# A decoder layer with two attention mixers: the second pair's queries and keys ahead of the transposed values, and the norm's sums inside the first pair's key product

## The chip, the cores and the metric

The kernel runs on one core of a Trainium2 chip. The metric is the device time of one execution in microseconds (us); three runs of the kernel before gave a median of 1153.85 us (1153.38 to 1154.62). The engines are named as the profile names them: PE (TensorE, matrix products; PEld is its weight load), DVE (VectorE), ACT (ScalarE), POOL (GpSimd) and SP (SyncE, which here only issues transfers). Each engine works through its own list of instructions in order and waits for others by semaphores.

## The reference, cut to what matters

```python
x = x + 0.5 * swiglu(rmsnorm(x, norm_ffn1), ffn1_gate, ffn1_up, ffn1_down)
h = rmsnorm(x, norm_mix)
qa, ka, va, qb, kb, vb, g_a, g_b = split(h @ w_in)      # 12 heads A, 8 heads B, 64 wide
# A: dilated windows, heads 0-3 (128, 1), 4-7 (512, 4), 8-11 (2048, 16); keys t - i*dilation
for each group: out, lse = dilated_window_attention(q, k, v, slopes, window, dilation)
y_a = sum(softmax(lse over the groups) * out)            # heads h, 4+h, 8+h merge into one
# B: block-sparse causal attention (at 512 positions every past block is taken)
y_b = moba_attention(qb, kb, vb, slopes)
merged = sigmoid(g_a) * (y_a @ w_up_a) + sigmoid(g_b) * (y_b @ w_up_b)
x = x + merged @ w_out
x = x + 0.5 * swiglu(rmsnorm(x, norm_ffn2), ffn2_gate, ffn2_up, ffn2_down)
return rmsnorm(x, norm_final)
```

There are 512 positions, a width of 1024 and an inner width of 2816, all float32; `rmsnorm` divides by the root of the mean square over the width and multiplies by a gain.

## The kernel before, in words

**Tiles.** The activations lie transposed: eight tiles `X[k]` of 128 features by 512 positions. A float32 product is made of three matmuls (`mac`, L205 to L210): both operands are split into a rounded high part and the rest, and high*high, high*low and low*high are summed in PSUM. One product of a 128-wide column of weights with all of `h` is eight such triples, 24 matmuls of 512 columns.

**Weights.** All weight tiles come in one list, `stream`, in the order in which the products ask for them. `fetch` loads a tile three ahead (tile `raw`, three buffers, queue of SP), `split` makes its high part on ACT (`whi`, L191) and the rest on DVE (`wlo`, L192) one tile ahead, in two buffers. A changed order of the products changes this list with them.

**The norm.** The gain is put on `X` before the products; the factor 1/root(mean square) of each position is multiplied onto the results afterwards, so products can start before it is known. `squares` sums the squares tile by tile into `SSQ`. `factors` (L245) splits the sum (`sh` on ACT, `sl` on DVE), adds over the 128 partitions by two matmuls with ones (L251, L252, into `ps_out`), and then works on DVE and ACT: mean (L256), root (L239, ACT), reciprocal (L240), a Newton step (L241, L242) and the factor as a row `rrow` (L243). `columns` (L265) takes it out as columns too.

**Queries, keys and values of the mixers.** `project` makes one product for a pair of heads, queries (j = 0) or keys (j = 1). `stacked` (L459) multiplies by `rrow` into the tile `qkv` (L466, one buffer), splits it into `qkhl` (two buffers; high part on ACT, L468, rest on DVE, L469), and copies high and low parts with SP's queue into the stacked tiles `qs` and `ks` that the scores read: four copies for queries (L480, 64x512), four for keys (L482, 64x1024). The second use of a `qkhl` buffer must wait until the copies out of it have landed. `values_by_class` (`vd`) makes a pair of the dilated heads' values, multiplies by `rrow` into `qkv` as well (L531), and `turned` transposes it by four matmuls with the identity (L541, 128x128), after which ACT and DVE split it into the tile `vd` (L544, L545). `turned` is called inside the next item's product, after 18 of its 24 matmuls (`LATER`), or, when no item follows, at the list's end.

**The order.** PE's instructions stand as the program writes them. `FIRST` lists what is done ahead of the first heads: pair 0 (heads 0 and 1, by hand, L774 to L782), then the rest of the list. `BESIDE` lists for each main stage (scores of a head, then its weighted sums) which products run beside it, mixed in by `blend`. The first head's scores (L578) need the queries and keys of pair 1 (heads 4 and 8) first, then (L590) those of pair 0; the third head's need those of pair 4 (heads 6 and 10). The lists of DVE, ACT and SP are made by a scheduler from the program's order and its own estimates.

Of the kernel before, what the change touches and what calls it, by code (L numbers as in the profile page):

```python
# [49 lines left out]
def slopes(n):  # L50
# [5 lines left out]
WAIT = 5  # L56
LEAD = 9
LATER = 5

FIRST = [("qk", 0), ("vd", 0), ("vd", 2), ("qk", 1)]
BESIDE = [
    [("qk", 2), ("v", 0)], [("qk", 3)],
    [("vd", 1), ("g", 0)], [("vd", 3), ("qk", 4), ("g", 1, 0)],
    [("qk", 5)], [("qk", 6)],
    [("g", 1, 1), ("v", 3)], [("qk", 7)],
    [("qk", 8)], [("v", 4)],
# [28 lines left out]
def decoder_layer(ctx: ExitStack, tc: tile.TileContext, xT, gains, gus, gu1, dn1, wqk, wv, wvd, wg, wup, wout, gu2, dn2, base, out):  # L97
# [11 lines left out]
    def bank(which):  # L109
        group = {"all": range(8), "acc": range(4), "att": (4, 5, 6), "out": (7,)}[which]  # L110
        n = turn[which] = turn.get(which, -1) + 1
        b = group[n % len(group)]
        return psum.tile([P, 512], F32, tag=f"b{b}", name=f"ps_{which}_{n}")

    def f32(ap):
        return ap.bitcast(F32)
# [26 lines left out]
    def mixer_tiles(what, n, *js):  # L143
        src = {"qk": lambda j: wqk[2 * n + j], "v": lambda j: wv[max(0, n - 2), j], "vd": lambda j: wvd[n], "g": lambda j: wg[2 * n + j]}[what]
        return [((what, n, j), src(j)) for j in js or range(1 if what == "vd" else 2)]

    def down_tiles(i, dn):
        return [((i, "d", m, c), dn[m][:, cut]) for m in range(KT) for c, cut in enumerate(CHUNKS)]
# [3 lines left out]
    stream += down_tiles(0, dn1)  # L152
    stream += [tile for items in [FIRST] + BESIDE for item in items for tile in mixer_tiles(*item)]
    for m in range(KT):
# [41 lines left out]
    def weights(*key):  # L196

        t = state["at"]
        assert stream[t][0] == key, (t, stream[t][0], key)
        state["at"] += 1  # L200
        split(t + 1)
        fetch(t + 3)
        return splits.pop(t)

    def mac(ps, w, x, first, last):  # L205

        (wh, wl), (xh, xl) = w, x
        nc.tensor.matmul(ps, wh, xh, start=first, stop=False)  # L208
        nc.tensor.matmul(ps, wh, xl, start=False, stop=False)  # L209
        nc.tensor.matmul(ps, wl, xh, start=False, stop=last)  # L210

    def cols(w, k, n=P):
        return w[0][:, k * n:(k + 1) * n], w[1][:, k * n:(k + 1) * n]
# [23 lines left out]
    def newton(y, z, a, out):  # L237

        nc.scalar.activation(y, a, AF.Sqrt)  # L239
        nc.vector.reciprocal(y, y)  # L240
        nc.vector.scalar_tensor_tensor(z, y, -0.5, y, ALU.mult, ALU.mult)  # L241
        nc.vector.tensor_tensor(z, z, a, ALU.mult)  # L242
        nc.vector.scalar_tensor_tensor(out, z, 1.5, y, ALU.add, ALU.mult)  # L243

    def factors(i, ps):  # L245

        sh = tpool.tile([P, S], F32R, name="sh", tag="fg")
        sl = tpool.tile([P, S], F32R, name="sl", tag="fu")
        nc.scalar.copy(sh, SSQ[i])
        nc.vector.tensor_tensor(sl, SSQ[i], f32(sh), ALU.subtract)  # L250
        nc.tensor.matmul(ps, ones_r, sh, start=True, stop=False)  # L251
        nc.tensor.matmul(ps, ones_r, sl, start=False, stop=True)  # L252
        a = tpool.tile([P, S], F32, name="mean", tag="fg")
        y = tpool.tile([P, S], F32, name="root", tag="fu")
        z = tpool.tile([P, S], F32, name="step", tag="ssq", bufs=1)
        nc.vector.tensor_scalar(a, ps, 1.0 / D, EPS, ALU.mult, ALU.add)  # L256
        row = tpool.tile([P, S], F32, name="rrow", tag="rrow", bufs=1)
        newton(y, z, a, row)
        return row

    def columns(row):

        rest = tpool.tile([P, P], F32, name="rest", tag="fu")
        for t in range(NT):
            nc.vector.tensor_tensor_reduce(rest, row[:, t * P:(t + 1) * P], ident, 1.0, 0.0, ALU.mult, ALU.max,  # L265
                                           accum_out=rcol[:, t:t + 1])
        return rcol
# [167 lines left out]
    with ExitStack() as mix:  # L435
        op = mix.enter_context(tc.tile_pool(name="op", bufs=2))
        att = ExitStack()
# [10 lines left out]
        R = {}  # L448
        Q, K = {}, {}

        def project(t, j, which="acc"):

            w = weights("qk", t, j)
            ps = bank(which)
            for k in range(KT):
                mac(ps, cols(w, k), XN[k], k == 0, k == KT - 1)
                yield ps

        def stacked(t, j, ps):  # L459
            v = tpool.tile([P, S], F32, name="qkv", tag="ssq", bufs=1)  # L460

            dilated = PAIRS[t][0] in range(NT, NA)
            to, x, r = v, ps, R["row"]
            if dilated:
                to, x, r = v.rearrange("p (r i) -> p r i", r=NT), by_class(x), by_class(r)
            nc.vector.scalar_tensor_tensor(to, x, -0.125 if j == 0 else 1.0, r, ALU.mult, ALU.mult)  # L466
            hl = mp2.tile([P, 2, S], F32R, name="qkhl", tag="qkhl", bufs=2)
            nc.scalar.copy(hl[:, 0], v)  # L468
            nc.vector.tensor_tensor(hl[:, 1], v, f32(hl[:, 0]), ALU.subtract)  # L469

            for n, h in enumerate(PAIRS[t]):
                s = slice(n * HD, (n + 1) * HD)
                if j == 0:
                    Q[h] = op.tile([P, S], F32R, name="qs", tag="qs", bufs=6)
                else:
                    K[h] = op.tile([P, 2, S], F32R, name="ks", tag="ks", bufs=6)
                for half in range(2):
                    d = slice(half * HD, (half + 1) * HD)
                    if j == 0:
                        nc.sync.dma_start(f32(Q[h][d]), f32(hl[s, half]))  # L480
                    else:
                        nc.sync.dma_start(f32(K[h][d]), f32(hl[s]))  # L482
# [53 lines left out]
        def turned():  # L536

            n, vt = TURN.pop()
            pt = bank("att")
            for r in range(NT):  # L540
                nc.tensor.transpose(pt[:, r * P:(r + 1) * P], vt[:, r * P:(r + 1) * P], ident)  # L541
            v = mp.tile([P, NT, 2, P], F32R, name=f"vd{n}", tag=f"vd{n}", bufs=1)
            x = pt.rearrange("p (r h c) -> p r h c", r=NT, h=2)
            nc.scalar.copy(v[:, :, :, :HD], x)  # L544
            nc.vector.tensor_tensor(v[:, :, :, HD:], x, f32(v[:, :, :, :HD]), ALU.subtract)  # L545
            for h in range(2):
                for r in range(NT):
                    V[r, 4 + 2 * n + h] = v[:, r, h]
# [203 lines left out]
        def part(what, n, *js):  # L752

            if what == "qk":
                return qk_pair(n), 2 * KT
            if what == "v":
                return values(n), NT * KT
            if what == "vd":
                return values_by_class(n), KT
            js = js or range(2)  # L760
            return (step for j in js for step in gate(n, j)), len(js) * KT

        def parts(items):

            for item in items:
                for at, _ in enumerate(part(*item)[0]):
                    if at == LATER and TURN:
                        turned()
                    yield
            if TURN:  # L770
                turned()
# [1 line left out]

        early = []  # L774
        for j in range(2):
            for ps in project(0, j, "att"):
                pass
            early.append(ps)
        R["row"] = factors(1, bank("out"))
        R["col"] = columns(R["row"])  # L780
        for j in range(2):
            stacked(0, j, early[j])  # L782
        for _ in parts(FIRST[1:]):
            pass
# [47 lines left out]
        for m in range(KT):  # L832
            w = weights("out", m)
            ps = bank("acc")
# [92 lines left out]
```

## Time and profile before

| | |
|---|---|
| median of three runs | 1153.85 us |
| the profiled execution | 1152.99 us |
| its span, first to last instruction | 1151.1 us |
| PE busy | 1126.2 us (98%) |
| DVE, ACT busy | 600.7 us (52%), 413.1 us (36%) |
| granted TensorE clock, mean | 0.990 |

The profile is of one execution. Times in it count from the span's start. A timeline row has the start, the duration, engine, line, operation, out<-in with buffer numbers left out, and in brackets how long the engine had been idle and what ended that. Matmuls overlap: the distance between two starts, not the duration, is what a row costs. [...] First layer half: to 366 us; mixers: about 366 us on.

### The profile page before, as it was taken

How to read it: one execution, taken by the hardware profiler on the slowest of the kernel's cores; microseconds unless marked ns; L12 is line 12 of the kernel's file. 1: busy time of each engine (PE TensorE's matmuls, PEld its weight loads, DVE VectorE, ACT ScalarE, POOL GpSimd, SP SyncE). 2: the span in 40 equal slices, each digit the busy share in tenths (PEclk: the TensorE clock that was granted, in tenths of full speed). 3: DMA queues.
4: the chain of work that ended last, by engine and by line, in shares of the span. 5: the costliest groups of instructions: out<-in, count | busy, mean ns of one | idle time of the engine just before them, and what ended most of it. 6: DMA issues, size and time to landing. Idle time of an engine off the chain costs nothing.

```text
span 1151.1 us, 13539 instructions
## 1 busy us (share of the span) xinstructions
PE 1126.2 (98%) x5332; PEld 944.4 (82%) x5332; DVE 600.7 (52%) x968; ACT 413.1 (36%) x637; POOL 20.0 (2%) x34
## 2 busy tenths in 40 slices
PE   9999999999999879999999999999999999999997
PEld 7888888888888659878998888888888888888886
DVE  6744444433333546757677667754744444433223
ACT  5432232222223234444455445433422322322222
POOL 0000000000000000000000000000000000000001
PEclk9999999999999889999999999999999999999999
DMA  6222322233333444436354212332223222333321
GB/s 220 92 92 99 102 92 95 99 91 101 101 89 127 128 127 131 128 110 169 109 162 128 74 65 83 114 106 92 92 97 103 93 93 100 101 86 98 101 83 73
DMA packets 37711, 122.14 MB, mean 106 GB/s; under 512 B 4880, under 2 KB 4880, under 8 KB 37648
## 3 DMA queue, kind: packets, MB, share of 16 engines
q1 hardware_dynamic: 37072, 120.08, 33.4%
q10 hardware_dynamic: 576, 1.20, 0.3%
q8 instruction: 42, 0.69, 0.2%
q14 instruction: 21, 0.17, 0.0%
HBM read 103.44 MB, written 2.10 MB: 92 GB/s over the span
## 4 chain that ended last, share of the span: by engine, by line
PE 95%; DVE 2%; DMA 2%; issue 0%; SPq 0%; ACT 0%; DVEq 0%; ACTq 0%
PE ps_all L208 20%; PE ps_all L210 20%; PE ps_all L209 20%; PE ps_acc L208 8%; PE ps_acc L210 8%; PE ps_acc L209 8%; PE ps_all L280 2%; PE ps_out L680 2%; PE ps_att L208 1%; PE ps_att L210 1%; PE ps_att L661 1%; PE ps_att L209 1%; DMA ks<-qkhl 1%; PE ps_att L636 1%; DMA raw<-in_wqk_dram 0%
## 5 line engine op out<-in xcount | busy, mean ns | idle before, releaser
L191 ACT CAST whi<-raw 128x1024 fp32r<-128x1024 f32 (+2 forms) x201 | 202.9, 1011 | 558.8 <-PE ps_all L209 255.0
L192 DVE TENSOR_TENSOR wlo<-raw,whi 128x1024 fp32r<-128x1024 f32 (+2 forms) x202 | 236.2, 1171 | 163.8 <-ACT whi L191 163.7
L210 PE MATMUL ps_all<-xh,wlo 128*128 128x512 f32 x672 | 261.5, 389 | 0.0
L209 PE MATMUL ps_all<-xl,whi 128*128 128x512 f32 x672 | 261.5, 389 | 0.0
L208 PE MATMUL ps_all<-xh,whi 128*128 128x512 f32 x672 | 261.5, 389 | 0.0
L209 PEld LDWEIGHTS ps_all<-xl,whi 128*128 128x128 f32 x672 | 126.1, 188 | 26.3
L210 PEld LDWEIGHTS ps_all<-xh,wlo 128*128 128x128 f32 x672 | 126.1, 188 | 26.1
L208 PEld LDWEIGHTS ps_all<-xh,whi 128*128 128x128 f32 x672 | 126.1, 188 | 26.1
L208 PE MATMUL ps_all<-ah,whi 128*128 128x512 f32 (+1 forms) x374 | 141.2, 378 | 0.0
L209 PE MATMUL ps_all<-al,whi 128*128 128x512 f32 (+1 forms) x374 | 140.8, 377 | 0.0
L210 PE MATMUL ps_all<-ah,wlo 128*128 128x512 f32 (+1 forms) x374 | 140.8, 377 | 0.0
L208 PE MATMUL ps_acc<-xh,whi 128*128 128x512 f32 x304 | 125.3, 412 | 0.0
L209 PE MATMUL ps_acc<-xl,whi 128*128 128x512 f32 x304 | 120.7, 397 | 0.0
L210 PE MATMUL ps_acc<-xh,wlo 128*128 128x512 f32 x304 | 120.6, 397 | 0.0
L294 DVE TENSOR_TENSOR fu<-ps_all,rrow 128x512 f32<-128x512 f32 x44 | 30.4, 690 | 124.2 <-PE ps_all L210 124.1
L208 PEld LDWEIGHTS ps_all<-ah,whi 128*128 128x128 f32 x374 | 70.4, 188 | 13.0
L209 PEld LDWEIGHTS ps_all<-al,whi 128*128 128x128 f32 x374 | 70.4, 188 | 12.9
L210 PEld LDWEIGHTS ps_all<-ah,wlo 128*128 128x128 f32 x374 | 70.4, 188 | 12.9
L292 DVE TENSOR_TENSOR fg<-ps_all,rrow 128x512 f32<-128x512 f32 x44 | 30.4, 690 | 79.8 <-PE ps_all L210 79.7
L210 PEld LDWEIGHTS ps_acc<-xh,wlo 128*128 128x128 f32 x304 | 58.2, 191 | 13.1
L209 PEld LDWEIGHTS ps_acc<-xl,whi 128*128 128x128 f32 x304 | 58.7, 193 | 8.5
L208 PEld LDWEIGHTS ps_acc<-xh,whi 128*128 128x128 f32 x304 | 58.5, 193 | 8.6
(169 smaller groups left out, 1186.6 us busy)
## 6 DMA issues: line engine op xcount, KB each, us to landing
raw<-in_gu_dram SPq DMA_DIRECT2D x84, 512.0 KB, 3.4
raw<-in_dn_dram SPq DMA_DIRECT2D x32, 512.0 KB, 3.5
raw<-in_wqk_dram SPq DMA_DIRECT2D x20, 512.0 KB, 3.5
ks<-qkhl SPq DMA_DIRECT2D x40, 256.0 KB, 4.8
raw<-in_wg_dram SPq DMA_DIRECT2D x16, 512.0 KB, 3.5
raw<-in_dn_dram SPq DMA_DIRECT2D x16, 384.0 KB, 3.1
qs<-qkhl SPq DMA_DIRECT2D x40, 128.0 KB, 2.4
raw<-in_wout_dram SPq DMA_DIRECT2D x8, 512.0 KB, 3.4
```

What stands on the lines that cost most here:

```text
L191: nc.scalar.copy(hi[:, s], raw[:, s])
L192: nc.vector.tensor_tensor(lo[:, s], raw[:, s], f32(hi[:, s]), ALU.subtract)
L208: nc.tensor.matmul(ps, wh, xh, start=first, stop=False)
L209: nc.tensor.matmul(ps, wh, xl, start=False, stop=False)
L210: nc.tensor.matmul(ps, wl, xh, start=False, stop=last)
L280: nc.tensor.matmul(ps[j], w[:, at:at + P], x, start=k == 0 and n == 0, stop=k == KT - 1 and n == 2)
L292: nc.vector.tensor_tensor(g, ps[0], R, ALU.mult)
L294: nc.vector.tensor_tensor(u, ps[1], R, ALU.mult)
L636: nc.tensor.matmul(ps[:, :n], Q[NA + h][:, i * P:(i + 1) * P], K[NA + h][:, part, :n], start=part == 0, stop=part == 1)
L661: nc.tensor.transpose(pt[:, n * P:(n + 1) * P], block, ident)
L680: nc.tensor.matmul(to(po), V[v], x[:, first:first + n], start=done == 1, stop=done == 2 * n_products)
```

## The change

It changes three places. `FIRST` now has pair 1's queries and keys right behind pair 0's, and the two products of transposed values (`vd` 0 and 2) behind them. In the stage of the second head's weighted sums, pair 4 stands ahead of `vd` 3. And `factors` is called inside pair 0's key product, after its second triple (`SUMS = 1`, counted from 0), not behind it. Nothing is added or taken out; both programs have 5106 rows in PE's list.

```diff
-FIRST = [("qk", 0), ("vd", 0), ("vd", 2), ("qk", 1)]
+SUMS = 1
+FIRST = [("qk", 0), ("qk", 1), ("vd", 0), ("vd", 2)]
 BESIDE = [
     [("qk", 2), ("v", 0)], [("qk", 3)],
-    [("vd", 1), ("g", 0)], [("vd", 3), ("qk", 4), ("g", 1, 0)],
+    [("vd", 1), ("g", 0)], [("qk", 4), ("vd", 3), ("g", 1, 0)],
...
         early = []
         for j in range(2):
-            for ps in project(0, j, "att"):
-                pass
+            for at, ps in enumerate(project(0, j, "att")):
+                if (j, at) == (1, SUMS):
+                    R["row"] = factors(1, bank("out"))
             early.append(ps)
-        R["row"] = factors(1, bank("out"))
         R["col"] = columns(R["row"])
```

Line numbers after the list rise by one (L541 becomes L542). PE at the two matmuls with ones, first before, then after; `ps_att_2592` is pair 0's key product, `ps_acc_2667` the product that follows it.

```order
L209 MATMUL ps_att_2592<-xl_7_2531,whi 128x512
L210 MATMUL ps_att_2592<-xh_7_2530,wlo 128x512
L251 MATMUL ps_out_2617<-sh,ones_r 128x512
L252 MATMUL ps_out_2617<-sl,ones_r 128x512
L208 MATMUL ps_acc_2667<-xh_0_1880,whi 128x512
```
```order
L210 MATMUL ps_att_2592<-xl_1_1973,whi 128x512
L211 MATMUL ps_att_2592<-xh_1_1972,wlo 128x512
L252 MATMUL ps_out_2599<-sh,ones_r 128x512
L253 MATMUL ps_out_2599<-sl,ones_r 128x512
L209 MATMUL ps_att_2592<-xh_2_2065,whi 128x512
```

The two rows with ones moved ahead by 18 rows, from behind the key product to its second triple; `xh_1` is the operand of that triple.

DVE, from pair 0's keys on, first before, then after. `ps_att_2592` is pair 0's keys; before, `ps_acc_2667` and `ps_acc_2700` are the transposed values and `ps_acc_2741` pair 1's queries; after, `ps_acc_2667` and `ps_acc_2709` are pair 1's queries and keys, and `ps_acc_2751` the first values.

```order
L466 SCALAR_TENSOR_TENSOR qkv<-ps_att_2592,rrow 128x512
L469 TENSOR_TENSOR qkhl<-qkv,qkhl 128x512
L531 TENSOR_TENSOR qkv<-ps_acc_2667,rrow 128x512
L545 TENSOR_TENSOR vd_2724<-ps_att_2719,vd_2724 128x8x64
L531 TENSOR_TENSOR qkv<-ps_acc_2700,rrow 128x512
L192 TENSOR_TENSOR wlo<-raw,whi 128x1024
L545 TENSOR_TENSOR vd_2765<-ps_att_2760,vd_2765 128x8x64
L466 SCALAR_TENSOR_TENSOR qkv<-ps_acc_2741,rrow 128x512
```
```order
L467 SCALAR_TENSOR_TENSOR qkv<-ps_att_2592,rrow 128x512
L470 TENSOR_TENSOR qkhl<-qkv,qkhl 128x512
L467 SCALAR_TENSOR_TENSOR qkv<-ps_acc_2667,rrow 128x512
L193 TENSOR_TENSOR wlo<-raw,whi 128x1024
L470 TENSOR_TENSOR qkhl<-qkv,qkhl 128x512
L467 SCALAR_TENSOR_TENSOR qkv<-ps_acc_2709,rrow 128x512
L470 TENSOR_TENSOR qkhl<-qkv,qkhl 128x512
L532 TENSOR_TENSOR qkv<-ps_acc_2751,rrow 128x512
L193 TENSOR_TENSOR wlo<-raw,whi 128x1024
L546 TENSOR_TENSOR vd_2808<-ps_att_2803,vd_2808 128x8x64
```

The splits of pair 1 (L467, L470) now stand right behind those of pair 0, and the first values' multiplication (L532) behind the split of pair 1's keys.

PE at the transposes, first before (inside the second values' product), then after (both, up to the first triple of pair 2's queries, `ps_acc_2833`).

```order
L209 MATMUL ps_acc_2700<-xl_5_2345,whi 128x512
L210 MATMUL ps_acc_2700<-xh_5_2344,wlo 128x512
L541 MATMUL ps_att_2719<-ident,qkv 128x128 x4
L208 MATMUL ps_acc_2700<-xh_6_2437,whi 128x512
L209 MATMUL ps_acc_2700<-xl_6_2438,whi 128x512
L210 MATMUL ps_acc_2700<-xh_6_2437,wlo 128x512
```
```order
L211 MATMUL ps_acc_2784<-xh_5_2344,wlo 128x512
L542 MATMUL ps_att_2803<-ident,qkv 128x128 x4
L209 MATMUL ps_acc_2784<-xh_6_2437,whi 128x512
L210 MATMUL ps_acc_2784<-xl_6_2438,whi 128x512
L211 MATMUL ps_acc_2784<-xh_6_2437,wlo 128x512
L209 MATMUL ps_acc_2784<-xh_7_2530,whi 128x512
L210 MATMUL ps_acc_2784<-xl_7_2531,whi 128x512
L211 MATMUL ps_acc_2784<-xh_7_2530,wlo 128x512
L542 MATMUL ps_att_2819<-ident,qkv 128x128 x4
L209 MATMUL ps_acc_2833<-xh_0_1880,whi 128x512
```

The first transposes still stand behind 18 rows of another product, now that of the second values (`ps_acc_2784`); the second ones, which stood 18 rows into pair 1's queries, stand directly behind the product whose result they read.

## Rows read from the trace of the kernel before

**Rows 1.** The page, parts 1 and 5: busy times; the weights' split on DVE.
```profile
PE 1126.2 (98%) x5332; PEld 944.4 (82%) x5332; DVE 600.7 (52%) x968; ACT 413.1 (36%) x637; POOL 20.0 (2%) x34
...
L192 DVE TENSOR_TENSOR wlo<-raw,whi 128x1024 fp32r<-128x1024 f32 (+2 forms) x202 | 236.2, 1171 | 163.8 <-ACT whi L191 163.7
```
**Rows 2.** Waits of PE, whole span: who for whom, us in total, times, longest.
```profile
PE ps_att L578 <- DMA ks<-qkhl: 9.1, 3, 6.1
PE ps_att L541 <- DVE qkv L531: 5.6, 1, 5.6
```
**Rows 3.** Timeline of PE: start, duration, line, operation; idle before it.
```profile
377.40 0.39 PE L251 MATMUL ps_out<-sh,ones_r 128*128 128x512 f32 x1
...
377.85 0.39 PE L208 MATMUL ps_acc<-xh,whi 128*128 128x512 f32 x1
...
387.15 0.39 PE L210 MATMUL ps_acc<-xh,wlo 128*128 128x512 f32 x1
...
393.17 1.09 PE L541 MATMUL ps_att<-ident,qkv 128*128 128x128 f32 x4 [5.64 <-DVE qkv L531]
...
400.83 0.60 PE L541 MATMUL ps_att<-ident,qkv 128*128 128x128 f32 x4
...
419.12 0.55 PE L578 MATMUL ps_att<-ks,qs 128*128 128x256 f32 x1 [1.48 <-DMA ks<-qkhl]
...
424.39 0.40 PE L578 MATMUL ps_att<-ks,qs 128*128 128x256 f32 x2
...
506.28 0.40 PE L210 MATMUL ps_acc<-xh,wlo 128*128 128x512 f32 x1
...
508.89 0.36 PE L578 MATMUL ps_att<-ks,qs 128*128 128x256 f32 x1 [1.54 <-DMA ks<-qkhl]
...
513.19 0.40 PE L578 MATMUL ps_att<-ks,qs 128*128 128x256 f32 x2
...
1140.36 0.61 PE L352 MATMUL ps_all<-ones,sql 128*128 128x1 f32 x4 [0.96 <-ACT sql L348]
```
**Rows 4.** Timelines of DVE and ACT, 366 to 442 us.
```profile
370.75 0.69 DVE L250 TENSOR_TENSOR sl<-ssq,sh 128x512 fp32r<-128x512 f32 x1 [0.69 <-ACT sh L249]
...
378.05 0.69 DVE L256 TENSOR_SCALAR mean<-ps_out 128x512 f32<-128x512 f32 x1 [3.77 <-PE ps_out L252]
...
380.78 3.35 DVE L240 RECIPROCAL root<-root 128x512 f32<-128x512 f32 x1 [0.90 <-ACT root L239]
...
386.64 0.68 DVE L243 SCALAR_TENSOR_TENSOR rrow<-step,root 128x512 f32<-128x512 f32 x1
...
391.25 0.69 DVE L469 TENSOR_TENSOR qkhl<-qkv,qkhl 128x512 fp32r<-128x512 f32 x1 [0.68 <-ACT qkhl L468]
...
391.98 1.05 DVE L531 TENSOR_TENSOR qkv<-ps_acc,rrow 128x512 f32<-128x512 f32 x1
...
396.86 1.08 DVE L531 TENSOR_TENSOR qkv<-ps_acc,rrow 128x512 f32<-128x512 f32 x1 [1.25 <-PE ps_acc L210]
...
390.60 0.62 ACT L468 CAST qkhl<-qkv 128x512 fp32r<-128x512 f32 x1 [1.58 <-DVE qkv L466]
```
**Rows 5.** Tile `ks`, stretches 391.9 to 395 and 411 to 414.4: issues; issue to landing.
```profile
L482 SPq DMA_DIRECT2D ks<-qkhl x4: 462/599/1206, 392.0 to 393.8; - x4
...
DMA to landing us min/median/max: 2.9/4.1/4.8
...
L482 SPq DMA_DIRECT2D ks<-qkhl x4: 461/698/1170, 411.1 to 413.2; - x4
...
DMA to landing us min/median/max: 4.7/5.5/5.9
```
**Rows 6.** Stretches: length, busy time (instructions) of five engines, granted clock, DMA share, GB/s.
```profile
420.00:425.00 5.00, 5.00 (x16) 3.96 (x15) 1.05 (x4) 1.21 (x3) 0.00 (x0) 0.59 0.00 0
...
510.00:512.00 2.00, 2.00 (x8) 1.63 (x7) 1.11 (x5) 0.94 (x3) 0.00 (x0) 0.50 0.04 8
...
1141.00:1142.00 1.00, 1.00 (x10) 1.00 (x10) 0.69 (x3) 0.20 (x1) 1.00 (x2) 1.00 0.56 217
```
## The prediction, made before the changed kernel was run

> **What bounds the kernel now.** I read the busy times first: PE is busy for 98% of the span [rows 1], so only two things can give time back, moments in which PE waits and stretches in which its clock is low. The list of PE's waits came next. Two are large, and both lie where the mixers begin: the transposes wait 5.6 us for the multiplied values, and the scores wait 9.1 us in three places for the copied keys [rows 2]. Then the timeline of PE between the first product that the change moves and the second row of scores. At full clock a row of 512 columns costs 0.227 us: from 377.85 to 387.15 there are 41 starts in 9.30 us [rows 3]. From 377.85 to the scores at 424.39 PE has 120 such rows (four products of 24 and the 24 rows of pair 2's queries), two groups of transposes (0.4 us each, an estimate between the 0.23 of their 4 x 128 columns and the 0.60 of the undisturbed group's duration) and one pair of 256-column scores (0.23). That is 27.2 + 0.8 + 0.2 = 28.2 us of work, and it took 46.5 us [rows 3]: 18.3 us too many. 13.2 of them are the waits (5.6, and 9.1 less the 1.5 of the wait at 508.89 [rows 2, 3]); the other 5 are work at a low clock, as after the second wait, where 420 to 425 was granted 0.59 [rows 6]. [...] So 22.3 us are to be had at most, and the change touches all of them.
>
> **The sums.** They stand at 377.40; 18 rows earlier is 373.3. Their input `sl` is ready at 370.75 + 0.69 = 371.4 [rows 3, 4], so PE doesn't wait and has 1.9 us to spare. Both rows remain, so PE's first moved product still starts at 377.85. The mean could start 4.1 us earlier than 378.05; I allow 0.2 for the weight split that DVE's list has ahead of it, and take 3.9. Between the mean and the row factor there is one weight split in either order (before, it stood ahead of L243, now behind the reciprocal), so the factor comes at 386.64 - 3.9 = 382.7 and the chain behind it moves alike [rows 4].
>
> **Pair 0's and pair 1's splits.** Pair 0's keys were split at 391.25 + 0.69 = 391.9 [rows 4]. 3.9 earlier is 388.1; one more weight split, 1.17 us on average [rows 1], now stands between, so 389.3. Then their four copies start. Before, the first was issued at 392.0 and the last landed at 393.8 + 4.8 = 398.6, 6.6 later [rows 5]; so they land at 395.9. This matters now and didn't before: there are two `qkhl` buffers, pair 1's queries and keys follow at once, and the cast of pair 1's keys must wait until pair 0's keys have left the same buffer. Its input is there sooner (the key product ends at 377.85 + 48 x 0.227 = 388.7, and the multiplications and the weight split ahead of it on DVE are through by about 393.5), so the copies decide. Cast 0.62 [rows 4], split 0.69 and 0.1 of hand-overs: 397.3. Queued behind that split on DVE is the first values' multiplication, for which PE's transposes wait: 1.05 us and 0.14 of hand-over, as between 391.98 and 393.17 [rows 3, 4], gives 398.5. PE reaches those transposes at 377.85 + 90 x 0.227 = 398.3. The 5.6 us become 0.2. The price of this step can't be below nothing, since a wait is no gain; its upper end, from the slower set of copies, 413.2 + 5.9 - 411.1 = 8.0 us [rows 5], is 1.6. I take 0.2, since that set had a weight load directly ahead of it in SP's list and pair 0's, as now, had its queries' copies.
>
> [...]
>
> **The second transposes.** These are a new wait, and a firm one: nothing stands between the second values' product and the transposes of its result. It is 0.16 (the last row's 0.39 less the 0.23 to the next start), 0.05, the multiplication's 1.08 [rows 4] and 0.14: 1.4 us. PE has nothing else in its list meanwhile. Its bounds are 1.2 and 1.6, by the two durations and the hand-overs; I take 1.4.
>
> **The first scores.** PE has 6 rows left after the first transposes, then waits 1.4, transposes again and does 12 rows of pair 2's queries: 398.5 + 0.4 + 1.4 + 1.4 + 0.4 + 2.7 = 404.8. Pair 1's keys are split at 397.3; with 6.6 us they are all there at 403.9, with 8.0 at 405.3 [rows 5]. A weight load stands ahead of them in SP's list, so I take 8.0: 0.5 us of wait in place of 7.6, with 0 as the other end. Behind it the 24 rows of pair 2's queries run at full clock.
>
> **The third head.** Pair 4's keys are finished 24 rows and a group of transposes earlier, 24 x 0.227 + 0.4 = 5.8 us. The scores asked for them at about 506.5 and got them at 508.9 [rows 3]; now they land near 503. The wait and the low clock behind it, 4.0 us, go, with over 3 us to spare. What moves behind is `vd` 3, whose values are first read by the third head's sums, a stage later; its split and the gate's multiplication come later on DVE, which may hold the first scores' rows there by 0 to 1 us. I take 0, since PE has three banks to go on with.
>
> **The sum.** 22.3 less 0.2, 1.4 and 0.5 is 20.2 us. Against the profiled execution's 1152.99 us (the span of 1151.1 and 1.9 around it) that gives 1132.8; the median of the runs was 0.86 above the profiled one, so I predict 1133.7 us.
>
> **Rivals.**
> 1. The short wait is enough to lower the clock. For it: the wait at the third head, 2.3 us with a short pair of scores inside it, was followed by 0.50 at 510 to 512; against it: after 0.96 us without work at 1140.36 the next stretch had 1.00 [rows 3, 6]. 1.4 lies between. Price: what low clock cost behind the two waits, 4.0 - 2.3 = 1.7 at the third head, and 424.39 - 419.12 less 0.1 and 12 x 0.227 = 2.4 at the first [rows 3]; the result would be 1135.4 to 1136.1. [...] No row here shows a wait of 1.4 us.
> 2. The copies of pairs 0 and 1, now close together on one queue, land late. Pair 0's by 8.0 instead of 6.6 adds 1.4 at the transposes and passes on to pair 1's; with the low clock of rival 1 added, since the first wait is then 1.6 and the second follows, 1135 to 1138. For it speaks that sixteen copies and two weight loads now follow one another in SP's list; against it, that pair 0's keys have hardly more directly ahead of them than before.
> 3. The third head's wait stays or a DVE queue takes its place: + 4.0, 1137.7. Against it speak the 3 us to spare.
> 4. The change doesn't do what it says at the sums: the factor is no earlier, since DVE or ACT is held by the weight splits. Then pair 0's keys land at 399.8, all behind them comes 3.9 later, with some 2 us of low clock: 1139.6.
> 5. Slower: pair 1's key split on DVE and ACT, waiting for pair 0's copies, holds the values, the weight splits and so all of PE. Each us by which the copies land after 395.7 costs one; it loses in the end only if they land 20 us after that, 26.8 us after their first issue. Rows have 6.6 and 8.0.
>
> **How the numbers follow.** Forecast 55% (its own range 1132.5 to 1135), rival 1 20%, rival 2 13%, rival 3 7%, rival 4 3%, rival 5 2%. Low end: all of 22.3 but the firm 1.4 is 1133.0 by the median, less 2 us for what the counted rows may miss: 1131. High end: rivals 1 to 4 reach 1139.6, so 1140. This kernel tells a change from none at about 0.2%, 2.3 us: every case but the last is faster by more. So faster 97%, same 1%, slower 2%.
>
> **What would show it.** In the profile after: the matmuls with ones at 373.3 without a wait, the row factor near 382.7; the cast of pair 1's keys beginning when pair 0's last copy lands, near 396; transposes near 398.5 with little wait and again near 401.7 with 1.4; the first scores complete near 405.3 instead of 419.1; a granted clock of 1.00 from 377 to 425; no wait at the third head's scores, and the rest shifted by the same amount. I am wrong if the first transposes wait over 2 us, if the clock falls to 0.50 behind the second, or if the distance from the row at 377.85 to the second row of scores is above 32 us.

## The result, and the profile after

The changed kernel took 1132.96 us, the median of four runs (1132.74 to 1133.19); the kernel before, run beside it, 1153.62 us (1153.14 to 1154.62). The ratio is 0.982, with a 95% interval of 0.9803 to 0.9837. The prediction was 1133.7 us with a range of 1131.0 to 1140.0, and faster with a chance of 0.97: right in sign, in size and in most of its steps. One term was too small by 1.1 us and another too large by 0.5. Of the experiments below, one execution of the kernel with the second transposes later took 1889.27 us at a mean granted clock of 0.557 and is left out of that kernel's median.

The page, part 1 (busy us, share of the span, instructions), against [rows 1]:

```profile
PE 1119.1 (99%) x5332; PEld 939.4 (83%) x5332; DVE 600.8 (53%) x968; ACT 413.7 (37%) x637; POOL 20.0 (2%) x34
```

The span is 1131.1 us (1151.1 before). No engine has more or less to do; PE's 1126.2 became 1119.1, mainly because its rows at half clock are gone (some 5 us at the mixers' beginning and 1.7 at the third head, by the prediction's count). The waits of PE, which answer to [rows 2] (who for whom, us in total, times, longest):

```profile
PE ps_att L542 <- DVE qkv L532: 2.3, 2, 1.2
PE ps_all L422 <- DVE wide L128: 1.5, 1, 1.5
```

Of 14.7 us in four places, 2.3 in two are left; PE no longer waits for keys. (The second row is at the program's start, and was there before.) The timeline of PE, which answers to [rows 3]. The zero point of this execution lies 0.74 us differently: the first moved product starts at 377.11 and not at 377.85.

```profile
372.58 0.39 PE L252 MATMUL ps_out<-sh,ones_r 128*128 128x512 f32 x1
...
377.11 0.39 PE L209 MATMUL ps_acc<-xh,whi 128*128 128x512 f32 x1
...
397.29 0.39 PE L211 MATMUL ps_acc<-xh,wlo 128*128 128x512 f32 x1
398.82 0.63 PE L542 MATMUL ps_att<-ident,qkv 128*128 128x128 f32 x4 [1.14 <-DVE qkv L532]
...
400.43 0.40 PE L211 MATMUL ps_acc<-xh,wlo 128*128 128x512 f32 x1
402.00 0.66 PE L542 MATMUL ps_att<-ident,qkv 128*128 128x128 f32 x4 [1.17 <-DVE qkv L532]
...
405.25 0.40 PE L579 MATMUL ps_att<-ks,qs 128*128 128x256 f32 x2
...
408.23 0.40 PE L579 MATMUL ps_att<-ks,qs 128*128 128x256 f32 x2
...
490.38 0.40 PE L579 MATMUL ps_att<-ks,qs 128*128 128x256 f32 x2
...
493.19 0.39 PE L579 MATMUL ps_att<-ks,qs 128*128 128x256 f32 x2
```

From the first moved product to the second row of scores it is 408.23 - 377.11 = 31.1 us where it was 46.5: 15.4 gained. From there to the fourth scores of the third head it is 493.19 - 408.23 = 85.0 us where it was 513.19 - 424.39 = 88.8 [rows 3]: 3.8 gained. That is 19.3 of the 20.0 us between the spans; the other 0.7 is the earlier start of this stretch, ahead of every edit. (In the eleven kernels of this study, equal up to there, `sl` starts between 370.02 and 370.75.) Stretches of the changed kernel (length, busy time of five engines, granted clock, DMA share, GB/s), which answer to [rows 6]:

```profile
388.00:396.00 8.00, 8.00 (x37) 6.63 (x36) 4.29 (x5) 1.68 (x2) 0.00 (x0) 1.00 0.97 251
398.00:403.00 5.00, 3.02 (x17) 2.37 (x18) 4.63 (x5) 1.95 (x3) 0.00 (x0) 1.00 0.90 216
403.00:425.00 22.00, 22.00 (x144) 20.09 (x143) 12.54 (x31) 10.37 (x23) 1.01 (x3) 1.00 0.58 172
490.00:495.00 5.00, 5.00 (x29) 4.23 (x27) 4.63 (x14) 1.95 (x7) 0.00 (x0) 1.00 0.32 105
```

The clock is 1.00 in all of them, also in the 5 us that hold both waits. How the first wait arises is read on DVE, ACT and the copies, which answer to [rows 4, 5]. DVE first:

```profile
381.97 0.69 DVE L244 SCALAR_TENSOR_TENSOR rrow<-step,root 128x512 f32<-128x512 f32 x1
...
387.63 0.69 DVE L470 TENSOR_TENSOR qkhl<-qkv,qkhl 128x512 fp32r<-128x512 f32 x1 [0.69 <-ACT qkhl L469]
...
396.82 0.69 DVE L470 TENSOR_TENSOR qkhl<-qkv,qkhl 128x512 fp32r<-128x512 f32 x1 [2.40 <-ACT qkhl L469]
397.62 1.05 DVE L532 TENSOR_TENSOR qkv<-ps_acc,rrow 128x512 f32<-128x512 f32 x1
```

ACT, the cast of pair 1's keys:

```profile
396.17 0.62 ACT L469 CAST qkhl<-qkv 128x512 fp32r<-128x512 f32 x1 [3.56 <-DMA ks<-qkhl]
```

Tile `ks`, the stretch of pair 0's four copies (386 to 392):

```profile
L483 SPq DMA_DIRECT2D ks<-qkhl x4: 461/712/1165, 388.3 to 390.4; - x4
...
DMA to landing us min/median/max: 4.5/5.3/5.7
```

The same for pair 1's (396 to 401):

```profile
L483 SPq DMA_DIRECT2D ks<-qkhl x4: 462/620/1164, 397.5 to 399.4; - x4
...
DMA to landing us min/median/max: 2.9/4.1/4.9
```

Read from the end: the transposes at 398.82 wait for the values' multiplication at 397.62, which stands in DVE's list behind the split of pair 1's keys at 396.82; that one waits for ACT's cast at 396.17, and the cast for pair 0's copies, the last of which was issued at 390.4 and landed 5.7 later, at 396.1. The chain is the predicted one. The copies took 7.7 us from the first issue (up to rounding), where 6.6 was planned.

### The profile page after: what moved, and what is told of

It reads as the page before. It is cut to its first block, busy times and chain, and to the rows that moved or that the text cites. A ratio compares the mean times of both kernels' runs of the same rounds, so it can differ in the third digit from the quotient of the medians.

```text
span 1131.1 us, 13533 instructions
## 1 busy us (share of the span) xinstructions
PE 1119.1 (99%) x5332; PEld 939.4 (83%) x5332; DVE 600.8 (53%) x968; ACT 413.7 (37%) x637; POOL 20.0 (2%) x34
## 4 chain that ended last, share of the span: by engine, by line
PE 96%; DVE 2%; DMA 1%; issue 0%; ACT 0%; SPq 0%; DVEq 0%; ACTq 0%
PE ps_all L210 21%; PE ps_all L209 21%; PE ps_all L211 21%; PE ps_acc L209 8%; PE ps_acc L211 8%; PE ps_acc L210 8%; PE ps_all L281 2%; PE ps_out L681 2%; PE ps_att L662 1%; PE ps_att L210 1%; PE ps_att L209 1%; PE ps_att L211 1%; PE ps_att L637 1%; DMA ks<-qkhl 1%; PE ps_all L422 0%
```

## The experiments

My theory for the time gained: three edits, each of which takes away waits and the low clock behind them, of which the sums matter mainly together with the new order. My theory for the 2.3 us left: the first wait is the buffer of `qkhl` held by pair 0's copies, the second is only PE having nothing else in its list.

**The swap alone.**

```diff
-    [("vd", 1), ("g", 0)], [("vd", 3), ("qk", 4), ("g", 1, 0)],
+    [("vd", 1), ("g", 0)], [("qk", 4), ("vd", 3), ("g", 1, 0)],
```

> The kernel before with one edit of the change alone: pair 4 ahead of the third transposed values in the stage of the second head's sums; the beginning of the mixers stays as it was. If the third head's wait was only a matter of order, the scores at 508.9 no longer wait, the granted clock there is 1.00 instead of 0.50, and all of the 4.0 us counted there are gained: about 1149.7. Rival A: the wait goes, but a row of DVE behind it becomes late (the gate's and the values' splits move back), and it costs up to 1 us: 1150.7. Rival B: the stage was covered anyway and the time stays within 0.5 us of 1153.6. The 5.6 and 7.6 us of wait at the mixers' beginning should be unchanged in all three.

1149.13 us against 1153.18, ratio 0.9967 (0.9955 to 0.9978): 4.05 us gained, 4.0 expected. PE's waits at the mixers' beginning stay (5.7 us for `qkv`, 7.8 for `ks`), and the third head's is gone, with a full clock there:

```profile
505.00:508.00 3.00, 3.00 (x17) 2.58 (x16) 2.90 (x6) 0.30 (x2) 0.00 (x0) 1.00 0.40 137
508.00:513.00 5.00, 5.00 (x27) 4.22 (x26) 4.28 (x18) 4.24 (x13) 0.00 (x0) 1.00 0.07 26
```

Neither a wait at the scores nor a stall of DVE takes its place. Its gain is about the same alone as in the changed kernel (3.8 us by the trace), so it is taken as independent of the others below.

**The sums alone.**

```diff
+                if (j, at) == (1, SUMS):
+                    R["row"] = factors(1, bank("out"))
             early.append(ps)
-        R["row"] = factors(1, bank("out"))
```

> The kernel before with only the two matmuls with ones moved 18 rows ahead. My theory: the row factor comes 3.9 us earlier, the wait of the first transposes falls from 5.6 to about 1.7, a wait of that length does not lower the clock (none of 1.2 us did in the changed kernel), so some 2.3 us of low clock behind it go too: 6.2 us, about 1147.4. The 7.6 us of wait for pair 1's keys stay, since they hang on when their product ends and not on the factor. Rival A: the wait for the keys grows by what is gained ahead of it, because the keys' split hangs on DVE's and ACT's lists, which did not begin earlier: within 1 us of 1153.6. Rival B: 1.7 us of wait is enough to lower the clock: only 3.9 us are gained, about 1149.7.

1150.0 us against 1153.18, ratio 0.9974 (0.9964 to 0.9983): 3.2 us gained, half of my 6.2. Rival A is false, since the wait for the keys did not grow (6.0 us in its longest, 6.1 before). Rival B is nearest in time, but its reason was not tested, because the wait is not 1.7. The waits:

```profile
PE ps_att L579 <- DMA ks<-qkhl: 9.2, 3, 6.0
PE ps_att L542 <- DVE qkv L532: 2.8, 1, 2.8
```

DVE in this kernel shows why 2.8:

```profile
382.25 0.69 DVE L244 SCALAR_TENSOR_TENSOR rrow<-step,root 128x512 f32<-128x512 f32 x1
...
384.46 1.22 DVE L193 TENSOR_TENSOR wlo<-raw,whi 128x1024 fp32r<-128x1024 f32 x1
...
387.90 0.69 DVE L470 TENSOR_TENSOR qkhl<-qkv,qkhl 128x512 fp32r<-128x512 f32 x1 [0.68 <-ACT qkhl L469]
```

A weight split of 1.22 us now lies between the factor and the split of pair 0's keys (from the start of one to the other 5.65 us, 391.25 - 386.64 = 4.61 before [rows 4]). The prediction had counted this split; my expectation forgot it. And 2.8 us of wait still brought the low clock:

```profile
391.00:394.00 3.00, 3.00 (x8) 2.32 (x8) 1.95 (x3) 1.11 (x2) 0.00 (x0) 0.50 1.00 243
```

So 2.8 of the 5.6 us of wait went, and hardly any of the low clock behind it.

**The first products' order alone.**

```diff
-FIRST = [("qk", 0), ("vd", 0), ("vd", 2), ("qk", 1)]
+FIRST = [("qk", 0), ("qk", 1), ("vd", 0), ("vd", 2)]
```

> The kernel before with only the order of the first products changed (pair 1 ahead of the transposed values); the sums stay late and the third head keeps its order. My theory: pair 0's keys are split 3.9 us later than in the changed kernel, so the split of pair 1's keys and the first values come 3.9 later: the first transposes wait 1.3 + 3.9 = 5.2 us, the clock falls behind them (some 2.3 us), the second transposes still wait about 1.3, the scores not at all or under 1 us, and the third head keeps its 4.0: 1133.0 + 3.9 + 2.3 + 4.0 = 1143.2. If the three edits add up, the gains are 4.0 + 6.2 + 10.4 = 20.6 of the 20.7 measured. Rival A: the edits overlap (without the early sums this order only moves the 7.6 us of wait from the scores to the transposes): less than 5 us, over 1148.5. Rival B: this order alone does nearly all (the late factor has slack behind pair 1's 48 rows): under 1139.

1144.19 us against 1153.18, ratio 0.9924 (0.9908 to 0.9941): 9.0 us gained, 10.4 expected, and both rivals missed. PE:

```profile
402.24 1.09 PE L541 MATMUL ps_att<-ident,qkv 128*128 128x128 f32 x4 [4.51 <-DVE qkv L531]
...
407.04 1.11 PE L541 MATMUL ps_att<-ident,qkv 128*128 128x128 f32 x4 [1.15 <-DVE qkv L531]
...
412.21 0.40 PE L578 MATMUL ps_att<-ks,qs 128*128 128x256 f32 x2
```

The first wait is 4.5 (5.2 expected), the second 1.15, the first scores don't wait. From the first transposes to the first scores it is 412.21 - 402.24 = 10.0 us, and 6.4 in the changed kernel: 3.5 us of low clock, where I had put 2.3:

```profile
403.00:411.00 8.00, 6.85 (x20) 5.06 (x19) 3.58 (x4) 3.50 (x4) 0.00 (x0) 0.50 0.64 172
```

The clock, once down, stayed down across the second wait and for the rows behind it. The three edits alone gain 4.05 + 3.2 + 9.0 = 16.2 us, together 20.7. The missing 4.4 is what the sums do only under the new order. There they are worth 1144.19 - 4.05 - 1132.96 = 7.2 us, with the swap's gain as it was alone: the wait of 4.5 becomes 1.14, behind which the clock no longer falls, and the 3.5 us of low clock go as a whole. Alone they gave 3.2: 5.6 became 2.8, and behind 2.8 the clock still fell.

**What holds the first transposes: a third buffer.** (To make room, a table of constants is cut to what is used and an unused tile left out.)

```diff
-            hl = mp2.tile([P, 2, S], F32R, name="qkhl", tag="qkhl", bufs=2)
+            hl = mp2.tile([P, 2, S], F32R, name="qkhl", tag="qkhl", bufs=3)
```

> The changed kernel with a third buffer for the split queries and keys (a table of constants is cut to what is used, and an unused 40-column tile is left out, so that it fits). My theory: the wait of the first transposes, 1.14 us in the changed kernel, comes from the cast of pair 1's keys, which waits until pair 0's key copies have left the buffer. With a third buffer the cast waits for pair 0's queries alone, which leave at 391.8: split near 394.7, first values multiplied by 396.5, PE there at 397.5, so no wait; the second transposes keep 1.2. About 1.2 us less than the changed kernel, 1131.8. Rival: DVE's and ACT's backlog of weight splits, not the copies, holds the values; then the wait stays near 1.1 and the time at 1133.0.

1132.15 us (1131.92 to 1132.38), ratio to the kernel before 0.9817 (0.9804 to 0.983). DVE, split of pair 1's keys and first values:

```profile
393.32 0.69 DVE L470 TENSOR_TENSOR qkhl<-qkv,qkhl 128x512 fp32r<-128x512 f32 x1 [0.73 <-ACT qkhl L469]
394.11 1.07 DVE L532 TENSOR_TENSOR qkv<-ps_acc,rrow 128x512 f32<-128x512 f32 x1
```

PE, both transposes:

```profile
397.89 0.60 PE L542 MATMUL ps_att<-ident,qkv 128*128 128x128 f32 x4
...
401.04 0.66 PE L542 MATMUL ps_att<-ident,qkv 128*128 128x128 f32 x4 [1.16 <-DVE qkv L532]
```

The split comes 3.5 us earlier although the copies landed as late as before (396.1), and the first wait is gone while the second stays. The distance from the sums to the second scores fell from 35.65 us in the changed kernel to 34.38. The theory holds; the rival, that DVE's and ACT's backlog holds the values, does not.

**The tiles' places alone**, without the third buffer.

```diff
-    cpool.tile([P, 40], F32, name="round")
-        consts = mp.tile([P, 1344], F32, name="consts", tag="consts")
+        consts = mp.tile([P, 1288], F32, name="consts", tag="consts")
```

> The changed kernel with only the cut of the constants and the tile left out that the third buffer needs: every tile behind them lies at another place in the memory, no instruction differs. Expected: the time and the waits of the changed kernel, 1133.0, first transposes 1.1, second 1.2. Rival: the places of the tiles matter by themselves (over 0.5 us either way), and the runs with a third buffer can't be read without this one.

1133.63 us (1133.27 to 1134.11), ratio 0.983 (0.9817 to 0.9843). The waits are 0.9 and 1.2, the distance from the sums to the second scores 35.49: at the place in question 0.2 us changed. The 0.67 us above the changed kernel stand elsewhere; the stretch begins 0.35 later, and whether the rest is the spread of the runs or the tiles' places was not told apart. The third buffer is faster than this kernel by 1.5 us.

**The second transposes later.**

```diff
-        def parts(items):
+        def parts(items, rest=True):
...
-            if TURN:
+            if rest and TURN:
                 turned()
...
-        for _ in parts(FIRST[1:]):
+        for _ in parts(FIRST[1:], False):
```

> The changed kernel with the second transposes taken from directly behind the product whose result they read to 18 rows later, inside pair 2's queries. My theory: their wait (1.17 us) is only PE having nothing else in its list meanwhile, so it goes and nothing takes its place: about 1.2 us less, 1131.8. Rival: the first scores, which come 1.2 us earlier for it, then wait for pair 1's keys (these landed 1.0 us before PE reached them in the changed kernel), and 0.2 us or more of it is given back, up to all of it if the copies come later: 1132.0 to 1133.0.

1132.90 us, the median of five runs (1132.16 to 1135.94), ratio 0.9829 (0.9816 to 0.9842): as the changed kernel. PE:

```profile
398.92 0.63 PE L542 MATMUL ps_att<-ident,qkv 128*128 128x128 f32 x4 [0.63 <-DVE qkv L532]
...
404.82 0.36 PE L579 MATMUL ps_att<-ks,qs 128*128 128x256 f32 x1 [1.05 <-DMA ks<-qkhl]
406.40 0.60 PE L542 MATMUL ps_att<-ident,qkv 128*128 128x128 f32 x4
```

The second transposes no longer wait, but the scores wait 1.05 us for pair 1's keys: the rival. The second wait had been covering these copies. The first wait, 0.63 us, differs from the 1.14 of the changed kernel although the edit does not touch what it waits for; the table behind the last experiment shows why.

**Both.** The edits are the two above.

> Both edits, the third buffer and the later second transposes. My theory: no wait of PE is left at the mixers' beginning; the two gains add up, 2.4 us less than the changed kernel, 1130.6, which beats both kernels. Rival: with both, PE reaches the first scores 2.4 us earlier, ahead of pair 1's copies (landed 1.0 us before PE got there); unless the copies come earlier too, 1.4 us of wait stands there and the time is that of one edit alone, 1131.8.

1131.2 us (1131.03 to 1132.14), ratio 0.9811 (0.9798 to 0.9824), the fastest of all: 1.8 us under the changed kernel, 2.4 under the one with the tiles' places alone. PE:

```profile
373.21 0.39 PE L252 MATMUL ps_out<-sh,ones_r 128*128 128x512 f32 x1
...
398.18 0.60 PE L542 MATMUL ps_att<-ident,qkv 128*128 128x128 f32 x4
...
402.74 0.40 PE L579 MATMUL ps_att<-ks,qs 128*128 128x256 f32 x2
404.36 0.60 PE L542 MATMUL ps_att<-ident,qkv 128*128 128x128 f32 x4
...
406.18 0.40 PE L579 MATMUL ps_att<-ks,qs 128*128 128x256 f32 x2
```

There is no wait left at the mixers' beginning. From the sums to the second scores it is 406.18 - 373.21 = 33.0 us, 2.7 less. The third buffer also sets pair 1's copies free earlier (issued from 395.9 on, landed at 402.6), just ahead of the scores, so the later transposes now pay.

**Why pair 0's copies took 7.7 us: another queue.**

```diff
-                        nc.sync.dma_start(f32(K[h][d]), f32(hl[s]))
+                        (nc.scalar if t == 0 else nc.sync).dma_start(f32(K[h][d]), f32(hl[s]))
```

> The changed kernel with pair 0's four key copies issued by ACT, on a queue of their own, instead of by SP. In the changed kernel the last of them landed 7.7 us after the first was issued, behind a weight load and two query copies on SP's queue. Theory A, the order of the one queue: without anything ahead of them they land about 2 us after their issue and 1.08 us apart, so near 393.5 to 394; the cast of pair 1's keys, the values and the first transposes follow and their 1.14 us of wait go: 1131.8. Theory B, the DMA engines are full (their share was 0.97 from 388 to 396): all of it has to go through whatever the queue, so the last copy lands at 396 +- 0.5 as before, the wait stays at 1.1 and the time at 1133.0 or a little above it, since ACT now issues (3 us of its list, beside waits that it has anyway).

1136.55 us, ratio 0.9856 (0.9839 to 0.9872): slower than the changed kernel. Tile `ks`, 386 to 392:

```profile
L483 ACTq DMA_DIRECT2D ks<-qkhl x4: 519/664/1178, 388.6 to 390.6; - x4
...
DMA to landing us min/median/max: 4.4/5.1/7.1
```

The last copy landed at 390.6 + 7.1 = 397.7, 9.1 us after the first issue: later, not sooner. Theory A is false. (Beside its 2 us from issue to landing: in the changed kernel the eight 256 KB stores of the result took 2.2 us in the median, and none of the copies into `ks` took under 2.9.) Theory B's reason holds, since the DMA share was 1.00 from 388 to 396, but not its numbers: it had the last copy at 396 +- 0.5 and a wait of 1.1 us. One thing more had changed: SP, rid of the copies, issued the next weight load at 390.84 (395.15 in the changed kernel), and this landed 5.6 us later, at 396.4, ahead of the last copy. That this load is what held up the last copy is likely, but was not tested by itself. PE's first transposes:

```profile
400.41 0.63 PE L542 MATMUL ps_att<-ident,qkv 128*128 128x128 f32 x4 [2.49 <-DVE qkv L532]
```

The stretch of the copies, and the one with both transposes:

```profile
388.00:396.00 8.00, 8.00 (x37) 6.62 (x36) 4.54 (x5) 1.68 (x2) 0.00 (x0) 1.00 1.00 268
400.00:404.00 4.00, 2.42 (x15) 1.86 (x15) 3.64 (x5) 1.63 (x2) 0.00 (x0) 1.00 0.94 214
```

In the profiled execution, 1134.57 us at a mean clock of 0.999, the clock stayed at 1.00 behind that wait of 2.49 us; the other three took 1136.15 to 1137.26 at 0.995 to 0.998. That the same wait lowered their clock is likely, but not shown, since they have no trace.

**The weight load among the copies.** One load is cut to an eighth.

```diff
-                nc.sync.dma_start(raws[t][:, :n], src)
+                c = n // 8 if stream[t][0] == ("qk", 2, 1) else n
+                nc.sync.dma_start(raws[t][:, :c], src[:, :c])
+                if c < n:
+                    nc.gpsimd.memset(raws[t][:, c:], 0.0)
```

> The changed kernel with one weight load, that of pair 2's keys, which lies among pair 0's copies, cut to an eighth of its bytes (64 KB of 512; the rest of the tile is filled with zeros by POOL, so those keys are wrong in value and nothing else changes). If the 448 KB ahead of them on the same DMA engines are what made pair 0's copies late, they land about 448 KB / 243 GB/s = 1.8 us earlier, near 394.2, and the first transposes' wait goes: 1131.8. If the copies are bound by their own issue or by the query copies, they still land near 396 and the wait stays at 1.1: 1133.0.

1132.81 us, ratio 0.9821 (0.9806 to 0.9835). Tile `ks`, 386 to 392:

```profile
L486 SPq DMA_DIRECT2D ks<-qkhl x4: 462/598/1230, 389.1 to 390.9; - x4
...
DMA to landing us min/median/max: 3.0/4.1/4.9
```

PE's first transposes:

```profile
398.49 0.63 PE L545 MATMUL ps_att<-ident,qkv 128*128 128x128 f32 x4 [0.30 <-DVE qkv L535]
```

The copies took 6.6 us (390.9 + 4.9 - 389.1, up to rounding), 1.1 less than in the changed kernel and not the 1.8 estimated at 243 GB/s (what the kernel with the sums alone moved from 391 to 394, at a share of 1.00). They land as they did in the kernel before, where no load lay among them (2.9/4.1/4.8 [rows 5]). The wait fell by 0.84 to 0.30. The time is that of the changed kernel within what can be told, not the 1131.8 expected; the distance from the sums to the second scores fell by 0.85.

Not all of this is the load's. In two other kernels that leave these copies as they are, they took 7.2 and 7.5 us, and the first wait was 0.63 and 0.91. What all of them share is the step from the copies to the wait. ACT's cast of pair 1's keys begins when the last of pair 0's copies has landed; counted from the first moved product (us):

| kernel | copies took | cast begins | first wait | difference |
|---|---|---|---|---|
| weight load cut | 6.6 | 395.83 - 377.63 = 18.20 | 0.30 | 17.90 |
| second transposes later | 7.2 | 396.27 - 377.74 = 18.53 | 0.63 | 17.90 |
| tiles' places alone | 7.5 | 396.31 - 377.49 = 18.82 | 0.91 | 17.91 |
| changed kernel | 7.7 | 396.17 - 377.11 = 19.06 | 1.14 | 17.92 |
| other queue | 9.1 | 397.77 - 377.36 = 20.41 | 2.49 | 17.92 |
| first products' order alone | 7.9 | 399.67 - 377.17 = 22.50 | 4.51 | 17.99 |

The wait follows the landing one for one, also where the edit leaves the copies as they were. So the load costs the copies 0.6 to 1.1 us and the wait 0.3 to 0.8.

## Why the prediction was right, step by step

- **The sums.** Planned at 373.3, the factor at 382.7. With the zero point 0.74 us apart, 372.58 and 381.97 are 373.3 and 382.7: exact, and without a wait.
- **Pair 0's and pair 1's splits.** This is the term that was mis-sized: 0.2 us planned (0.1 by its own rows, since 391.94 - 3.9 is 388.0 and not 388.1); from the last row to the transposes 398.82 - 397.29 - 0.23 = 1.3. The mechanism and the chain were right, and the bounds of 0 to 1.6 held it. I had taken 6.6 us of the two sets of copies on the ground that hardly more lay ahead of pair 0's keys than before. But I had not followed SP's list: the load of the weights for pair 2's keys now stands between pair 0's query copies (issued at 385.66 us, landed 5.1 later), and the key copies behind it took 7.7. Rival 2 had named this, with a price of 1.4 at 8.0 us. Without that load the copies took 6.6 us and the wait was 0.30: the planned number, for the planned copies.
- **The values behind the copies.** The prediction had each us by which the copies land late cost one (rival 5), since the first values' multiplication stands behind the split of pair 1's keys in DVE's list. The traces agree: in the changed kernel DVE stood idle for 2.40 us ahead of that split and began the multiplication only behind it, at 397.62; with the third buffer the split came at 393.32 and the multiplication at 394.11. Over six kernels the wait is the start of the cast less 17.9 to 18.0 us, for waits from 0.30 to 4.51.
- **The second transposes.** 1.4 planned, 402.00 - 400.43 - 0.23 = 1.34 measured.
- **The first scores.** 0.5 planned with copies of 8.0 us; they took 6.7 (397.5 to 399.4 + 4.9, up to rounding) and landed at 404.3, 1 us before PE came. I had put the slower set on pair 1 and the faster on pair 0; it was nearer the other way round.
- **The third head.** 4.0 planned: from 506.28 to 513.19 it is 6.91 us, and 13 rows at 0.227 us are 2.95 [rows 3]. 3.8 from the trace, and 4.05 by the swap alone.
- **The sum.** 2.1 us were planned to remain; 1.3 + 1.34 = 2.6 of wait did. By the trace the change gained 19.3 us, 0.9 less than planned; that the time came out 0.7 us below the forecast and not above it is due to the earlier start of the stretch and the spread of the runs, not to the argument.
- **Rival 1**, that the short wait lowers the clock, did not occur: waits of 1.14 and 1.17 us, 3.2 apart, left the clock at 1.00, as did the waits of 1.16 us with the third buffer, of 0.63 and 1.05 with the second transposes later and of 0.30 and 1.2 with the weight load cut (1.00 in each stretch of 2 us from 398 to 406); behind 2.81 us, with the sums alone, it fell to 0.50. The length of one wait does not decide alone, though. 2.49 us left the clock at 1.00 in the profiled execution with the other queue, while at the third head of the kernel before a wait of 0.33 us, one matmul of scores and the wait of 1.54 us [rows 3] together were followed by 0.50 [rows 6]; so the prediction was right to fear it. What decides between these was not tested. The first of the two waits:

```profile
507.00 0.36 PE L578 MATMUL ps_att<-ks,qs 128*128 128x256 f32 x1 [0.33 <-PE ps_acc L210]
```

- **Rival 2** occurred in part: pair 0's copies were late by 1.1 of its 1.4 us, but neither the delay of the first scores nor the low clock that it had added followed. Rivals 3 to 5 did not occur.

## What to carry to other kernels

Price a wait with the low clock behind it, and look for edits that make it as short as those behind which the trace shows no fall (here single waits of up to 1.2 us): the last microseconds can be worth more than the first, and edits that each help little alone can help much together (here the sums brought 3.2 us alone and 7.2 under the new order). When copies decide a term, list everything that the same DMA engines carry around them, in the order of the issuing queue, before choosing a duration; when the engines are full, as here at a share of 0.97 to 1.00, another queue need not help (with it the copies took 9.1 us in place of 7.7). A wait that seems free to remove may be covering another one, as here one of 1.05 us, so remove both or neither.

## What was not expected of the hardware

- Pair 0's four key copies, 256 KB each and one behind another, landed 1.1 us apart in the changed kernel (from 388.3 + 4.5 to 390.4 + 5.7 it is 3.3 us for three), with the DMA engines' share at 0.97 and 251 GB/s in that stretch. Issued from another queue they were not faster: the last of them came 9.1 us after the first issue in place of 7.7, behind a weight load that the change of queue had let in.
- The clock's low stretch is not a fixed price. 3.5 us were lost behind a wait of 4.5 us that was followed by one of 1.15; the same second wait, at full clock, cost nothing but itself.
